# Mixer modulation split between TensorE and VectorE, in a hybrid decoder block on one Trainium2 core

## The chip, the core and the metric

The kernel runs on one core of one Trainium2 chip. Its five engines run their own instruction queues in order: TensorE (PE, with its weight loads as PEld), VectorE (DVE), ScalarE (ACT), GpSimd (POOL) and SyncE (SP), which here issues nearly all DMAs. The metric is device microseconds of one execution; lower is better.

## The reference

One decoder layer with adaptive normalisation over 512 tokens of width D = 2048, all in float32:

```python
mod = silu(c) @ w_ada + b_ada          # c: one row of 2048; w_ada: 2048 x 6*2048
sh_a, sc_a, g_a, sh_m, sc_m, g_m = split(mod, 6)
h    = rmsnorm(x, norm_mix_g) * (1 + sc_a) + sh_a
proj = h @ w_in                        # q_a k_a v_a | q_b k_b v_b f_b
...                                    # sliding-window and forgetting attention, w_out, two-level MoE, final norm
```

What matters here are the first two of the six sections of `mod`, the mixer's shift and scale: a row of 2048 times a 2048 x 4096 part of w_ada, 33.5 MB that are read once. Every column of h, and with it every row of w_in that is multiplied, waits for its own shift and scale.

## The kernel before

The first 150 us are one pipeline over the 2048 columns of h. The columns are cut into 8 "u" of 256, and these into UNITS ((0,1), (1,3), (3,5), (5,7), (7,8)). For each unit (loop over UNITS, L410):

- `gemv(u0, u1)` forms shift (sec 0) and scale (sec 1) of the unit's columns. For each section it loads w_ada in four row chunks kc (tiles `raws`, 1 MB each, five buffers in rotation, two of them the buffers of x) and multiplies each by silu(c) with 16 matmuls in four column groups of 32 (L318, `gv`). Silu(c) is the stationary operand, so all 32 rows of a group hold the same sum. ACT copies `gv` to `row` (L324), PE picks one row of each group, adds the four and turns them into columns (`cp`, L330), and VectorE writes shA (L332) or scA (L334, L335).
- `make_h(u0, u1)` scales the columns of x (already transposed in `xT`) by scA and by the token norm `rsb` (VectorE, L341), ACT adds the shift and rounds to the high part hT_hi (L342), VectorE forms the low part hT_lo (L345). Two column blocks k of 128 belong to each u.
- `start_proj(u0, u1)` is the projection of the finished unit: six steps for each u (two for the K piece of w_in, four for the Q piece), each step six matmuls of 512 columns (high x high, high x low, low x high, L211 to L213). A piece is fetched with `ws.get()`, which also issues loads ahead and lets ACT and VectorE cut the next piece into high and low parts (L172/L173 for K, L178/L179 for Q).

The projection of a unit runs inside the gemv of the next one: gemv is a generator that yields after each kc (yield 1) and after the copy of `row` (yield 0), and at each yield the loop takes n steps of `prev`, the projection of the unit before. What is left is emitted behind make_h. So the order on PE and on VectorE is written out by hand: an instruction that waits holds everything behind it on its engine. After the last unit, the K accumulators are copied out by ACT (L471, L472), and attention starts.

Before the units, `begin()` (L251) loads and transposes x, forms the token norms and spreads them over the partitions (`rb`, copied to `rsb` by ACT, L277); `columns()` (L279) transposes the small vectors (`vt`, copied to `vecs` by VectorE at L284, then `gps`, which uses the same PSUM bank).

Of the kernel before, what the change touches and what calls it, by code (L numbers as in the profile page):

```python
# [8 lines left out]
F32 = mybir.dt.float32  # L9
# [44 lines left out]
def kernel(  # L54
# [8 lines left out]
    V, S, G, PE, SP = nc.vector, nc.scalar, nc.gpsimd, nc.tensor, nc.sync  # L63
# [19 lines left out]
    big = ctx.enter_context(tc.tile_pool(name="big", bufs=1))  # L83
    frt = ExitStack()
    fr = frt.enter_context(tc.tile_pool(name="front", bufs=1, side="right"))
    att = ExitStack()
    sb = att.enter_context(tc.tile_pool(name="start", bufs=1))
    pst = ExitStack()
    ps = pst.enter_context(tc.tile_pool(name="ps0", bufs=1, space=PSUM, reuse_waits="tile"))
# [15 lines left out]
    ones = ones1.to_broadcast([128, 128])  # L105
    sel4 = big.tile([128, 1], F32, name="sel4")
    V.memset(sel4, 0.0)
    for q in range(4):
        V.memset(sel4[32 * q:32 * q + 1, :], 1.0)
    csig = big.tile([128, 4, 4], F32, name="csig")  # L110
    S.activation(csig, ccol, AF.Exp, scale=-1.0)
    V.tensor_scalar(csig, csig, 1.0, None, op0=OP.add)
    V.reciprocal(csig, csig)
    csil = big.tile([128, 4, 4], F32, name="csil")
    V.tensor_mul(csil, ccol, csig)
    cs32 = big.tile([128, 16, 32], F32, tag="wr", name="cs32")
    V.tensor_copy(cs32, flat(csil)[:, :, None].to_broadcast([128, 16, 32]))

    shA = big.tile([128, 16], F32, name="shA")
    scA = big.tile([128, 16], F32, name="scA")  # L120
# [3 lines left out]
    def rsqrt_(dst, v, tmp):  # L124

        S.activation(tmp, v, AF.Sqrt)
        V.reciprocal(dst, tmp)
        V.tensor_mul(tmp, dst, dst)
        V.tensor_mul(tmp, tmp, v)
        V.tensor_scalar(tmp, tmp, -0.5, 1.5, op0=OP.mult, op1=OP.add)  # L130
        V.tensor_mul(dst, dst, tmp)  # L131
# [83 lines left out]
    hT_hi = fr.tile([128, 4, 4, T], F32R, tag="B", name="hT_hi")  # L215
    hT_lo = [big.tile([128, 4 * n, T], F32R, tag=f"C{i}", name=f"hT_lo{i}") for i, n in enumerate((3, 1))]

    def kt(ts, k, sl=slice(0, T)):

        return ts[k // 12][:, k % 12, sl]  # L220
# [10 lines left out]
    xT = [sb.tile([128, 4, T], F32, name=f"xT{i}") for i in range(4)]  # L231
    rsb = fr.tile([128, T], F32, tag="gacc1", name="rsb", bufs=1)
# [18 lines left out]
    def begin():  # L251

        for tb in range(TB):
            SP.dma_start(xt[tb], x[tb * 128:(tb + 1) * 128, :])
        scr = fr.tile([128, 2, 1024], F32, tag="ga", name="sqscr")
        for tb in range(TB):
            V.tensor_tensor_reduce(scr[:, 0], xt[tb][:, :1024], xt[tb][:, :1024], scale=1.0, scalar=0.0, op0=OP.mult,
                                   op1=OP.add, accum_out=sx2[:, tb, 0:1])
            S.activation(scr[:, 1], xt[tb][:, 1024:], AF.Square, accum_out=sx2[:, tb, 1:2])
            for i in range(4):  # L260
                tr = ps.tile([128, 4, 128], F32, tag=f"acc{(4 * tb + i) % 6}", name=f"xTp_{tb}_{i}")
                for j in range(4):
                    k = 4 * i + j
                    PE.transpose(tr[:, j, :], xt[tb][:, k * 128:(k + 1) * 128], ident)
                o = xT[i][:, :, tb * 128:(tb + 1) * 128]
                if i % 2:
                    V.tensor_copy(o, tr)
                else:
                    S.activation(o, tr, AF.Copy)
        V.tensor_reduce(ssx, sx2, axis=AX.X, op=OP.add)  # L270
        V.tensor_scalar(ssx, ssx, 1.0 / D, EPS, op0=OP.mult, op1=OP.add)
        rsqrt_(rsx, ssx, tsx)
        rb = ps.tile([128, T], F32, tag="tr", name="rb")
        for tb in range(TB):
            PE.matmul(rb[:, tb * 128:(tb + 1) * 128], rsx[:, tb:tb + 1].to_broadcast([128, 128]), ident,
                      start=tb == 0, stop=tb == TB - 1)
        S.activation(rsb, rb, AF.Copy)  # L277

    def columns():  # L279

        vt = ps.tile([128, 2, 24], F32, tag="tr", name="vt")
        for j in range(2):
            PE.transpose(vt[:, j, :], vrow[:, 128 * j:128 * j + 128], ident[:24, :24])
        V.tensor_copy(vecs.rearrange("p n (u j) -> p n u j", j=2), vt.rearrange("p j (n u) -> p n u j", n=3))  # L284
        gps = ps.tile([128, 16], F32, tag="tr", name="gps")
        PE.transpose(gps, grow, ident[:16, :16])
        V.tensor_copy(gout, gps)


    UNITS = ((0, 1), (1, 3), (3, 5), (5, 7), (7, 8))  # L290
    nraws = [0]

    def raws():

        n = nraws[0]
        nraws[0] += 1
        tag = f"raws{n % 3}" if n < 4 else ("raws1", "raws2", "A0", "A1", "raws0")[(n - 4) % 5]
        pool = sb if tag[0] == "r" else big
        return pool.tile([128, 4, 512], F32, tag=tag, name="raws", bufs=1)

    def gemv(u0, u1):

        n = 256 * (u1 - u0)
        ks = slice(2 * u0, 2 * u1)
        per = 512 // n
        for sec, dst in ((0, shA), (1, scA)):
            gv = ps.tile([128, 512], F32, tag="gv", name=f"gv_{sec}_{u0}")[:, :n]
            cols = slice(sec * D + u0 * 256, sec * D + u1 * 256)
            for kc in range(4):
                if kc % per == 0:  # L310
                    t = raws().rearrange("p a (b f) -> p (a b) f", f=n)
                    for i in range(2):
                        if per == 2:
                            SP.dma_start(t[:, 4 * i:4 * i + 4], rows4(w_ada, kc + i)[:, :, cols])
                        else:
                            SP.dma_start(t[:, 2 * i:2 * i + 2], rows4(w_ada, kc)[:, 2 * i:2 * i + 2, cols])
                for q in range(4):
                    PE.matmul(gv[32 * q:32 * q + 32, :], cs32[:, kc * 4 + q, :], t[:, kc % per * 4 + q, :],  # L318
                              start=kc == 0, stop=kc == 3)
                if sec and kc in (1, 3):  # L320
                    ws.ahead(2 * u0 + 2 if kc == 1 else 2 * u1)
                yield 1
            row = sb.tile([128, 512], F32, tag="bias", name=f"row_{sec}_{u0}", bufs=2)[:, :n]
            S.activation(row, gv, AF.Copy)  # L324
            if sec == 1 and u0 == 0:
                ws.split(2)
            yield 0
            cp = ps.tile([128, 512], F32, tag="tr", name=f"cp_{sec}_{u0}")[:, :n // 128]
            for k in range(n // 128):
                PE.matmul(cp[:, k:k + 1], row[:, k * 128:(k + 1) * 128], sel4, start=True, stop=True)  # L330
            if sec == 0:
                V.tensor_add(shA[:, ks], cp, vecs[:, 0, ks])  # L332
            else:
                V.scalar_tensor_tensor(scA[:, ks], cp, 1.0, vecs[:, 1, ks], op0=OP.add, op1=OP.add)  # L334
                V.tensor_mul(scA[:, ks], scA[:, ks], gmix[:, ks])  # L335

    def make_h(u0, u1):
        for k in range(2 * u0, 2 * u1 + 1):
            if k < 2 * u1:
                v = xT[k // 4][:, k % 4, :]  # L340
                V.scalar_tensor_tensor(v, v, scA[:, k:k + 1], rsb, op0=OP.mult, op1=OP.mult)  # L341
                S.activation(hT_hi[:, k // 4, k % 4, :], v, AF.Identity, bias=shA[:, k:k + 1])  # L342
            if k > 2 * u0:
                i, j = divmod(k - 1, 4)
                V.scalar_tensor_tensor(kt(hT_lo, k - 1), xT[i][:, j, :], shA[:, k - 1:k], hT_hi[:, i, j, :].bitcast(F32),  # L345
                                       op0=OP.add, op1=OP.subtract)

    WO = tuple((lambda cc=cc, n=n: wout_load(cc, n), False)
               for cc, ns in ((0, range(4)), (1, range(4)), (2, range(8)), (0, range(4, 8)), (1, range(4, 8)), (3, range(8)))
# [33 lines left out]
    ws = Stream(items)  # L383
# [25 lines left out]

    for g, us in enumerate(UNITS):  # L410
        if g == 1:
            S.dma_start(bfg, bcast(b_forget, 16))
            S.dma_start(sinkb, bcast(sinks, 16))
        if g == 0:
            begin()
            columns()
            acc0 = [ps.tile([128, 512], F32, tag=f"acc{i}", name=f"acc0_{i}") for i in range(6)]

        free = 6 * (UNITS[g - 1][1] - UNITS[g - 1][0]) - 4 if g else 0
        loads = 0  # L420
        for kc in gemv(*us):
            loads += kc
            n = 1
            if kc:
                n = free * loads // 8 - free * (loads - 1) // 8
            for _ in range(n):
                next(prev, None)
        make_h(*us)
        for _ in prev:
            pass  # L430
        prev = start_proj(*us)
# [795 lines left out]
    for tb in range(TB):  # L1227
        for k in range(tb + 1):
            PE.matmul(rk[:, tb, :], before if k == tb else ones_b, chosen_b[:, k].rearrange("p g e -> p (g e)"),
                      start=k == 0, stop=k == tb)  # L1230
# [468 lines left out]
```

## Time and profile before

| | us |
|---|---|
| median of 3 runs | 1908.92 |
| lowest, highest | 1907.39, 1909.3 |
| the profiled execution | 1906.88 |
| its span, first to last instruction | 1904.9 |
| PE busy in the span | 1811.7 (95%) |
| DVE busy | 1017.2 (53%) |
| ACT busy | 747.3 (39%) |

Times inside the kernel are us from the start of the span. The stretch that the change touches ends at 152; the rest of the span (attention, output projection, MoE) is untouched. "Granted clock" is the share of TensorE's full clock that it was given: 1.00 is 2.4 GHz, 0.50 is 1.2 GHz.

### The profile page before, as it was taken

How to read it: one execution, taken by the hardware profiler on the slowest of the kernel's cores; microseconds unless marked ns; L12 is line 12 of the kernel's file. 1: busy time of each engine (PE TensorE's matmuls, PEld its weight loads, DVE VectorE, ACT ScalarE, POOL GpSimd, SP SyncE). 2: the span in 40 equal slices, each digit the busy share in tenths (PEclk: the TensorE clock that was granted, in tenths of full speed). 3: DMA queues.
4: the chain of work that ended last, by engine and by line, in shares of the span. 5: the costliest groups of instructions: out<-in, count | busy, mean ns of one | idle time of the engine just before them, and what ended most of it. 6: DMA issues, size and time to landing. Idle time of an engine off the chain costs nothing.

```text
span 1904.9 us, 25988 instructions
## 1 busy us (share of the span) xinstructions
PE 1811.7 (95%) x9777; PEld 1130.0 (59%) x9777; DVE 1017.2 (53%) x1799; ACT 747.3 (39%) x1450; POOL 289.1 (15%) x217
## 2 busy tenths in 40 slices
PE   7998999999999999998899999999999999999995
PEld 4467888788777777777544454444444445444432
DVE  3334666666666544756645464444554545545435
ACT  3225656565565543345533232232331323323213
POOL 0000334444345241355000000000000000000000
PEclk8999999999999999999899999999999999999998
DMA  9963555565656332667899999999999999999995
GB/s 338 384 229 75 156 182 151 159 212 156 188 172 188 122 133 67 219 206 288 347 363 387 419 420 420 420 419 419 419 418 420 414 420 419 418 420 416 420 412 214
DMA packets 196501, 573.81 MB, mean 301 GB/s; under 512 B 22624, under 2 KB 86152, under 8 KB 147600
## 3 DMA queue, kind: packets, MB, share of 16 engines
q1 hardware_dynamic: 195456, 572.00, 79.3%
q8 instruction: 79, 1.29, 0.3%
q14 instruction: 54, 0.44, 0.1%
q10 hardware_dynamic: 912, 0.07, 0.0%
HBM read 567.82 MB, written 4.19 MB: 300 GB/s over the span
## 4 chain that ended last, share of the span: by engine, by line
PE 75%; DMA 8%; DVE 7%; ACT 6%; issue 3%; POOL 0%; SPq 0%; ACTq 0%; DVEq 0%; POOLq 0%
PE pu L1334 12%; PE pg L1334 11%; PE y L1356 9%; PE xe L1467 7%; PE o L1378 5%; DMA w<-in_w_up_dram 4%; PE qp L211 3%; PE qp L213 2%; PE qp L212 2%; DMA raw<-in_w_ada_dram 2%; PE acc L211 1%; PE gv L318 1%; PE acc L212 1%; PE acc L213 1%; PE ob L813 1%
## 5 line engine op out<-in xcount | busy, mean ns | idle before, releaser
L1334 PE MATMUL pu<-w,cw 128*64 128x512 f32 x1024 | 239.2, 593 | 5.4 <-DMA w<-in_w_up_dram 5.4
L1334 PE MATMUL pg<-w,cw 128*64 128x512 f32 x1024 | 236.2, 598 | 0.7 <-DMA w<-in_w_gate_dram 0.7
L1476 ACT ACTIVATE cw<-xe,shM,scM 128x128 f32<-128x128 f32 x128 | 58.5, 457 | 430.9 <-PE xe L1467 399.9
L1356 PE MATMUL y<-w,more_f 128*64 128x512 f32 x960 | 212.6, 594 | 4.3 <-ACT xp_whi L1448 2.4
L1474 DVE TENSOR_SCALAR cw<-xe,scM,shM 128x128 f32<-128x128 f32 x128 | 52.5, 410 | 300.7 <-ACT cw L1476 300.7
L612 POOL TENSOR_TENSOR gb<-gb,raw 128x512 f32<-128x512 f32 x112 | 162.2, 1448 | 276.1 <-ACT raw L611 210.8
L1381 DVE SCALAR_TENSOR_TENSOR x<-o,wpair,x 128x512 f32<-128x512 f32 x240 | 163.2, 743 | 19.4 <-PE o L1378 19.4
L1334 PEld LDWEIGHTS pu<-w,cw 128*64 128x64 f32 x1024 | 75.8, 137 | 154.0 <-issue 141.2
L1448 ACT ACTIVATE xp_whi<-x,rs 128x256 fp32r<-128x256 f32 x236 | 162.4, 761 | 1.1 <-DVE rs L131 1.1
L1356 PEld LDWEIGHTS y<-w,more_f 128*64 128x64 f32 x960 | 71.5, 137 | 132.8 <-issue 107.1
L1334 PEld LDWEIGHTS pg<-w,cw 128*64 128x64 f32 x1024 | 71.7, 136 | 131.4 <-issue 126.9
L173 DVE TENSOR_TENSOR wlo_s<-raw,whi_s 128x512 fp32r<-128x512 f32 x96 | 91.5, 954 | 107.2 <-ACT whi_s L172 107.0
L1454 DVE SCALAR_TENSOR_TENSOR xp_wlo<-x,rs,xp_whi 128x256 fp32r<-128x256 f32 x232 | 144.6, 682 | 2.2 <-ACT xp_whi L1448 2.2
L1467 PE MATMUL xe<-cr,xp_whi 128*128 128x256 f32 x472 | 121.9, 296 | 2.4 <-DVE cr L1437 2.4
L609 DVE SCALAR_TENSOR_TENSOR ga<-raw,csil,ga 128x512 f32<-128x512 f32 x112 | 109.5, 978 | 25.2 <-DMA raw<-in_w_ada_dram 24.7
L1467 PEld LDWEIGHTS xe<-cr,xp_whi 128*128 128x128 f32 x472 | 89.9, 190 | 49.5 <-issue 45.4
L1467 PE MATMUL xe<-cr,xp_wlo 128*128 128x256 f32 x472 | 115.6, 283 | 0.0
L211 PE MATMUL qp<-hT_hi,whi_s 128*128 128x512 f32 x256 | 107.7, 421 | 0.0
L213 PE MATMUL qp<-hT_hi,wlo_s 128*128 128x512 f32 x256 | 100.8, 394 | 0.0
L212 PE MATMUL qp<-hT_lo,whi_s 128*128 128x512 f32 x256 | 100.8, 394 | 0.0
L611 ACT ACTIVATE raw<-raw,csil 128x512 f32<-128x512 f32 x112 | 79.7, 713 | 31.8 <-DMA raw<-in_w_ada_dram 29.8
L1467 PEld LDWEIGHTS xe<-cr,xp_wlo 128*128 128x128 f32 x472 | 90.1, 191 | 0.0
(440 smaller groups left out, 3366.1 us busy)
## 6 DMA issues: line engine op xcount, KB each, us to landing
w<-in_w_gate_dram SPq DMA_DIRECT2D x128, 1024.0 KB, 10.7
w<-in_w_up_dram SPq DMA_DIRECT2D x128, 1024.0 KB, 14.0
w<-in_w_down_dram SPq DMA_DIRECT2D x126, 1024.0 KB, 10.3
raw<-in_w_ada_dram SPq DMA_DIRECT2D x128, 512.0 KB, 3.9
raws<-in_w_ada_dram SPq DMA_DIRECT2D x64, 512.0 KB, 10.2
raw<-in_w_in_dram SPq DMA_DIRECT2D x160, 128.0 KB, 3.0
raw<-in_w_out_dram SPq DMA_DIRECT2D x32, 512.0 KB, 3.8
raw<-in_w_in_dram SPq DMA_DIRECT2D x48, 256.0 KB, 3.6
```

What stands on the lines that cost most here:

```text
L211: PE.matmul(o, lhi, rhi, start=first, stop=False, **kw)
L212: PE.matmul(o, lhi, rlo, start=False, stop=False, **kw)
L213: PE.matmul(o, llo, rhi, start=False, stop=last, **kw)
L609: V.scalar_tensor_tensor(a, ts[n][:, j, :], s, a, op0=OP.mult, op1=OP.add)
L612: G.tensor_add(a, a, ts[n][:, j, :])
L1334: PE.matmul(o[64 * e:64 * e + 64, :], self.xe(cc)[:, j, 64 * e:64 * e + 64], w[cc, e][:, j, :], start=cc == 0 and j == 0, stop=cc == 3 and ...
L1356: PE.matmul(ys[dc][64 * e:64 * e + 64, :], HT[:, k, 64 * e:64 * e + 64], self.wd[k, e][:, dc, :], start=k == 0, stop=k == 3)
L1378: PE.matmul(o, self.ohT[:, tb, :], v, start=i == 0, stop=i == 1)
L1381: V.scalar_tensor_tensor(x2, o, self.w_col(tb), x2 if self.n else x1[dc][:, tb, :], op0=OP.mult, op1=OP.add)
L1448: S.activation(hi[tb], xv, AF.Identity, scale=s)
L1454: V.scalar_tensor_tensor(lo[tb], xv, s, hi[tb].bitcast(F32), op0=OP.mult, op1=OP.subtract)
L1467: PE.matmul(t[:, j, :], v[tb][:, j, :], OHS[:, tb].rearrange("p q s -> p (q s)"), start=tb + i == 0, stop=tb + i == TB)
```

## The change

For every unit but the first, the row chunks kc 0 and 1 are no longer multiplied on PE. VectorE multiplies each of their eight 128-row slices by the matching column of silu(c) and adds it up in a tile `sums`; PE adds `sums` over the partitions, 128 columns in each of up to four column groups (`st`, stationary operand ones), ACT copies that too, and one more matmul with `pick4` brings it into `cp`. So half of the multiplication by silu(c) moves from PE to VectorE, eight slices for each section.

UNITS becomes ((0,1), (1,3), (3,5), (5,6), (6,7), (7,8)). `raws` rotates over seven buffers, all four of x among them. The steps of the projection are dealt out by another rule: one at each yield as long as more than one is left, two of them kept for the yields 0. For a previous unit of two u it is one at each of the eight yields 1, one at each yield 0 and two behind make_h; for one u, a step at the first three yields 1, one at each yield 0, one behind make_h.

x is multiplied by the token norm ahead, in four VectorE instructions of 128x2048 in `norm_row()`, which with `columns()` now stands behind the first section of the first unit. make_h then needs one tensor_scalar (scale and shift together), one ACT copy and one subtraction for each k.

```diff
@@ begin / norm_row
+    def norm_row():
         rb = ps.tile([128, T], F32, tag="tr", name="rb")
...
         S.activation(rsb, rb, AF.Copy)
+        for i in range(4):
+            V.tensor_mul(xT[i], xT[i], rsb[:, None, :].to_broadcast([128, 4, T]))
@@
-    UNITS = ((0, 1), (1, 3), (3, 5), (5, 7), (7, 8))
+    UNITS = ((0, 1), (1, 3), (3, 5), (5, 6), (6, 7), (7, 8))
...
-        tag = f"raws{n % 3}" if n < 4 else ("raws1", "raws2", "A0", "A1", "raws0")[(n - 4) % 5]
+        tag = f"raws{n % 3}" if n < 4 else ("A0", "raws1", "A1", "raws2", "A2", "raws0", "A3")[(n - 4) % 7]
@@ gemv
+        se = 2 if u0 else 0
...
                 for q in range(4):
-                    PE.matmul(gv[32 * q:32 * q + 32, :], cs32[:, kc * 4 + q, :], t[:, kc % per * 4 + q, :],
-                              start=kc == 0, stop=kc == 3)
-                if sec and kc in (1, 3):
-                    ws.ahead(2 * u0 + 2 if kc == 1 else 2 * u1)
-                yield 1
+                    v = t[:, kc % per * 4 + q, :]
+                    if kc >= se:
+                        PE.matmul(gv[32 * q:32 * q + 32, :], cs32[:, kc * 4 + q, :], v, start=kc == se, stop=kc == 3)
+                    elif kc or q:
+                        V.scalar_tensor_tensor(sums, v, csil[:, kc, q:q + 1], sums, op0=OP.mult, op1=OP.add)
+                    else:
+                        V.tensor_scalar(sums, v, csil[:, 0, 0:1], None, op0=OP.mult)
+                if kc < 3:
+                    yield 1
+            st = ps.tile([128, 132], F32, tag="tr", name=f"st_{sec}_{u0}")
+            w = 32 * nk
+            for k in range(nk if se else 0):
+                PE.matmul(st[32 * k:32 * k + 32, :128], ones[:, 0:32], sums[:, k * 128:(k + 1) * 128], start=True, stop=True)
+            if sec:
+                ws.ahead(2 * u1)
+            yield 1
...
+            if se:
+                S.activation(row[:w, 512:], st[:w, :128], AF.Copy)
...
+            cp = st[:, 128:128 + nk]
+            if se:
+                PE.matmul(cp, row[:w, 512:], pick4[:w, :nk], start=True, stop=False)
+            for k in range(nk):
+                PE.matmul(cp[:, k:k + 1], row[:, k * 128:(k + 1) * 128], sel4, start=not se, stop=not se or k == nk - 1)
@@ make_h
-                V.scalar_tensor_tensor(v, v, scA[:, k:k + 1], rsb, op0=OP.mult, op1=OP.mult)
-                S.activation(hT_hi[:, k // 4, k % 4, :], v, AF.Identity, bias=shA[:, k:k + 1])
+                V.tensor_scalar(v, v, scA[:, k:k + 1], shA[:, k:k + 1], op0=OP.mult, op1=OP.add)
+                S.activation(hT_hi[:, k // 4, k % 4, :], v, AF.Copy)
...
-                V.scalar_tensor_tensor(kt(hT_lo, k - 1), xT[i][:, j, :], shA[:, k - 1:k], hT_hi[:, i, j, :].bitcast(F32),
-                                       op0=OP.add, op1=OP.subtract)
+                V.tensor_sub(kt(hT_lo, k - 1), xT[i][:, j, :], hT_hi[:, i, j, :].bitcast(F32))
@@ the loop over UNITS
-        free = 6 * (UNITS[g - 1][1] - UNITS[g - 1][0]) - 4 if g else 0
+        left = 6 * (UNITS[g - 1][1] - UNITS[g - 1][0]) - 2 if g else 0
         loads = 0
         for kc in gemv(*us):
             loads += kc
-            n = 1
-            if kc:
-                n = free * loads // 8 - free * (loads - 1) // 8
+            if g == 0 and kc and loads == 4:
+                norm_row()
+                columns()
+            n = (left + 8 - loads) // (10 - loads) if kc else 1
+            left -= n if kc else 0
             for _ in range(n):
                 next(prev, None)
```

## Rows read from the trace of the kernel before

**Rows 1.** Windows of the first stage: us, then each engine's busy us; PEclk, DMA share, GB/s.
```profile
20.00:37.00 17.00, 13.92 (x91) 5.63 (x91) 4.47 (x11) 4.06 (x8) 0.00 (x0) 0.51 0.96 321
37.00:58.00 21.00, 16.57 (x75) 5.20 (x70) 1.80 (x4) 1.60 (x4) 0.00 (x0) 0.99 1.06 382
58.00:120.00 62.00, 62.00 (x336) 37.22 (x335) 22.27 (x39) 16.77 (x27) 0.00 (x0) 1.00 1.06 378
120.00:152.00 32.00, 32.00 (x182) 21.95 (x180) 13.59 (x25) 13.31 (x23) 2.03 (x7) 1.00 0.25 65
```
**Rows 2.** Timeline of PE: start us, us, what; last data of unit (1,3), its scale.
```profile
56.73 1.05 PE L318 MATMUL gv<-raws,cs 128*32 128x512 f32 x4 [0.32 <-DMA raws<-in_w_ada_dram]
...
60.61 0.95 PE L330 MATMUL cp<-sel,row 128*128 128x1 f32 x8
```
**Rows 3.** Timeline of PE: gemv blocks and projection steps, later, and the end of the stage.
```profile
76.87 1.06 PE L318 MATMUL gv<-raws,cs 128*32 128x512 f32 x8
...
79.46 1.06 PE L318 MATMUL gv<-raws,cs 128*32 128x512 f32 x8
...
122.35 0.64 PE L318 MATMUL gv<-raws,cs 128*32 128x256 f32 x8
...
124.50 0.64 PE L318 MATMUL gv<-raws,cs 128*32 128x256 f32 x8
...
145.10 0.39 PE L211 MATMUL acc<-hT_hi,hi_s 128*128 128x512 f32 x1
...
146.49 0.39 PE L211 MATMUL acc<-hT_hi,hi_s 128*128 128x512 f32 x1
...
155.74 0.39 PE L211 MATMUL vaa<-hi_s,hT_hi 128*128 128x272 f32 x1 [3.60 <-ACT hi_s L172]
```
**Rows 4.** Timeline of VectorE: make_h of unit (3,5), and a Q piece behind it.
```profile
89.50 0.16 DVE L334 SCALAR_TENSOR_TENSOR scA<-cp,vecs 128x4 f32<-128x4 f32 x1 [3.64 <-PE cp L330]
...
89.89 1.42 DVE L341 SCALAR_TENSOR_TENSOR xT<-xT,scA,rsb 128x512 f32<-128x512 f32 x2
91.44 0.75 DVE L345 SCALAR_TENSOR_TENSOR hT_lo<-xT,shA,hT_hi 128x512 fp32r<-128x512 f32 x1
...
95.64 1.28 DVE L179 TENSOR_TENSOR lo_s<-raw,hi_s 128x512 fp32r<-128x512 f32 x2
```
**Rows 5.** Groups by line and shape of VectorE, 0 to 200 us: busy us, mean ns.
```profile
L607 DVE TENSOR_SCALAR ga<-raw,csil 128x512 f32<-128x512 f32 x1 | 0.5, 481 | 0.0
```
**Rows 6.** Timeline of VectorE, later: a 1024-wide subtraction; two dependent instructions.
```profile
860.26 1.22 DVE L173 TENSOR_TENSOR lo_s<-raw,hi_s 128x1024 fp32r<-128x1024 f32 x1
...
889.06 0.69 DVE L1095 TENSOR_TENSOR gx<-oq,ga 128x512 f32<-128x512 f32 x1 [1.28 <-PE oq L213]
889.79 0.69 DVE L1096 TENSOR_TENSOR x<-x,gx 128x512 f32<-128x512 f32 x1
```
**Rows 7.** Timeline of all engines: token norm, small vectors and gemv of the first unit.
```profile
20.20 0.60 ACT L277 ACTIVATE rsb<-rb 128x512 f32<-128x512 f32 x1 [2.26 <-PE rb L275]
...
21.56 0.28 PE L286 MATMUL gps<-ident,grow 16*128 16x16 f32 x1 [0.30 <-DVE vecs L284]
21.77 3.64 PE L318 MATMUL gv<-raws,cs 128*32 128x256 f32 x32
...
31.89 0.38 ACT L324 ACTIVATE row<-gv 128x256 f32<-128x256 f32 x1 [6.02 <-PE gv L318]
...
34.63 0.15 DVE L334 SCALAR_TENSOR_TENSOR scA<-cp,vecs 128x2 f32<-128x2 f32 x1
```
**Rows 8.** Windows (columns as in rows 1): the clock behind the pause that ends at 155.74.
```profile
157.00:158.00 1.00, 1.00 (x6) 1.00 (x5) 0.59 (x2) 0.97 (x2) 0.00 (x0) 0.50 0.37 53
...
161.00:162.00 1.00, 1.00 (x10) 1.00 (x9) 0.99 (x2) 0.78 (x2) 0.00 (x0) 1.00 0.00 0
```
**Rows 9.** Timeline of PE: a later pause.
```profile
189.16 0.39 PE L211 MATMUL vb<-whi_s,hT_hi 128*128 128x256 f32 x1 [2.80 <-ACT whi_s L172]
```
**Rows 10.** Windows: the clock behind that pause.
```profile
191.00:192.00 1.00, 1.00 (x7) 1.00 (x7) 0.74 (x4) 0.43 (x2) 0.00 (x0) 0.50 0.78 222
```

More of the change, by code (lines that the diff above doesn't have):

```diff
@@ L109 @@
         V.memset(sel4[32 * q:32 * q + 1, :], 1.0)
+    pick4 = big.tile([128, 4], F32, name="pick4")
+    V.memset(pick4, 0.0)
+    for q in range(4):
+        V.memset(pick4[32 * q:32 * q + 1, q:q + 1], 1.0)
     csig = big.tile([128, 4, 4], F32, name="csig")
@@ L304, in gemv @@
         ks = slice(2 * u0, 2 * u1)
-        per = 512 // n
+        per, nk = 512 // n, n // 128
+        se = 2 if u0 else 0
         for sec, dst in ((0, shA), (1, scA)):
             gv = ps.tile([128, 512], F32, tag="gv", name=f"gv_{sec}_{u0}")[:, :n]
+            if se:
+                sums = fr.tile([128, 2048], F32, tag="ga", name=f"sums_{sec}_{u0}")[:, :n]
             cols = slice(sec * D + u0 * 256, sec * D + u1 * 256)
@@ L317, in gemv @@
                 for q in range(4):
-                    PE.matmul(gv[32 * q:32 * q + 32, :], cs32[:, kc * 4 + q, :], t[:, kc % per * 4 + q, :],
-                              start=kc == 0, stop=kc == 3)
-                if sec and kc in (1, 3):
-                    ws.ahead(2 * u0 + 2 if kc == 1 else 2 * u1)
-                yield 1
-            row = sb.tile([128, 512], F32, tag="bias", name=f"row_{sec}_{u0}", bufs=2)[:, :n]
-            S.activation(row, gv, AF.Copy)
+                    v = t[:, kc % per * 4 + q, :]
[14 more added lines that the diff above has]
+            yield 1
+            row = sb.tile([128, 640], F32, tag="bias", name=f"row_{sec}_{u0}", bufs=2)
+            S.activation(row[:, :n], gv, AF.Copy)
+            if se:
+                S.activation(row[:w, 512:], st[:w, :128], AF.Copy)
             if sec == 1 and u0 == 0:
@@ L327, in gemv @@
             yield 0
-            cp = ps.tile([128, 512], F32, tag="tr", name=f"cp_{sec}_{u0}")[:, :n // 128]
-            for k in range(n // 128):
-                PE.matmul(cp[:, k:k + 1], row[:, k * 128:(k + 1) * 128], sel4, start=True, stop=True)
+            cp = st[:, 128:128 + nk]
+            if se:
+                PE.matmul(cp, row[:w, 512:], pick4[:w, :nk], start=True, stop=False)
+            for k in range(nk):
+                PE.matmul(cp[:, k:k + 1], row[:, k * 128:(k + 1) * 128], sel4, start=not se, stop=not se or k == nk - 1)
             if sec == 0:
@@ L415 @@
             begin()
-            columns()
             acc0 = [ps.tile([128, 512], F32, tag=f"acc{i}", name=f"acc0_{i}") for i in range(6)]
-        free = 6 * (UNITS[g - 1][1] - UNITS[g - 1][0]) - 4 if g else 0
+        left = 6 * (UNITS[g - 1][1] - UNITS[g - 1][0]) - 2 if g else 0
         loads = 0
```

## The prediction

> **What bounds the kernel now.** I read the windows first, since the change touches only the first 152 us. Up to 37 PE has gaps and a granted clock of 0.51; from 37 to 58 the DMA share is 1.06 and PE is busy 16.6 of 21.0 us; from 58 on PE has no gap, to 120 with DMA full as well, from 120 to 152 with DMA at 0.25 [rows 1]. So DMA sets the time up to the last data of unit (1,3), at 56.7 [rows 2], and PE alone from there to its last projection matmul at 152.1, 3.6 before 155.74 [rows 3]. VectorE is busy 22.3 of 62 us there [rows 1]: it looks free for more, and the question is whether its new work comes in time, because PE and VectorE both run in the order written. All later work follows the K accumulators through ACT, so I carry a shift of this stage to the end of the program in full.
>
> The anchor is the matmuls `cp` for the scale of unit (1,3): they start at 60.6 and end at 61.4 [rows 2]; before, the stage needs 152.1 - 61.4 = 90.7 us from there.
>
> **Prices of PE.** A step is 146.49 - 145.10 = 1.39. A 512-wide gemv block between steps costs 79.46 - 76.87 - 1.39 = 1.20, a 256-wide one 124.50 - 122.35 - 1.39 = 0.76 [rows 3]. `cp` for four columns costs about 0.9 [rows 2], for two half of it, 0.45. New in each section: the `st` matmuls, 128 wide, next to a gemv block in the same column groups. Half the width saves 0.44, so a quarter of the width would be about 0.55 with the switch to and from column groups and less without: I take 0.35, between 0.1 and 0.55. The matmul with `pick4` is one of the eight-for-0.9 kind, two passes, 0.2.
>
> **What PE loses and gains behind the anchor.** Unit (3,5): two sections, each without two blocks and with 0.55 more: 2 x (2.40 - 0.55) = 3.7 saved. Before, (5,7) costs 8 x 1.20 + 2 x 0.9 = 11.4; as (5,6) and (6,7) it costs four sections of 2 x 0.76 + 0.55 + 0.45 = 2.5, 10.1: 1.3 saved. Unit (7,8): 8 x 0.76 + 0.9 = 7.0 becomes 5.0: 2.0 saved. One projection step now lies ahead of the anchor: 1.4. Together 8.4 us less PE work; if PE never waited, the stage would end that much earlier.
>
> **Prices of VectorE.** Two instructions that don't depend on each other start 0.67 apart though each takes 0.75 [rows 4]; two that do start 0.73 apart at 0.69 each, the duration and 0.04 [rows 6]. Every addition to `sums` reads the one before, so I take 0.79 for 512 columns. The first of a section is a tensor_scalar, 0.48 [rows 5]. A 512-wide section: 0.52 + 7 x 0.79 = 6.05 (by 0.67 it would be 5.2). For 256 columns, half of the step from 0.69 to 1.22 between 512 and 1024 [rows 4, 6] comes off, 0.27: 0.52 each, 4.0 for a section (3.1 by the lower price). The Trainium skill, VectorE: DVE Perf Modes (section The DRAIN you can't avoid) says that the next instruction does not start until the pipe is empty; by that any two would be a full 0.75 apart. The pair in the trace at 0.67 shows that this holds only for dependent ones here; the sum would go by 5.8 a section.
>
> make_h gets shorter. Before, from scA to the end of the fourth low part: 95.6 - 89.5 = 6.1 [rows 4]. After, the tensor_scalar takes 0.48 (lower bound nothing, upper bound 0.75 as now), and the chain scale, ACT copy, subtraction gives the first low part 2.3 after `cp` (before, 92.2 - 89.5 = 2.7 behind the start of scA alone [rows 4]) and the fourth about 4.9 after it.
>
> **Where PE waits.** VectorE's order for a unit is: make_h, slices of kc 0, cutting of the Q piece that the first step asks for (1.28 [rows 4]), slices of kc 1. PE's order: two or one left steps, step 1, step 2, block kc 2, step 3, block kc 3, `st`. Step 3 needs the Q piece and `st` needs kc 1. Times in us behind the `cp` of the scale before:
> - Unit (3,5), shift: make_h ends at 4.9, kc 0 at 7.8, Q at 9.1, kc 1 at 12.3. PE has one left step and waits for the first low part until 2.3; then step 1 and 2 and a block, 6.3; step 3 waits to 9.2; with block kc 3 it is at 11.8, and `st` waits 0.5. Waits: 0.9 + 2.9 + 0.5. The scale section has enough steps: no wait.
> - Unit (5,6), shift: four k in make_h still, narrow slices. Kc 0 ends at 6.9, Q at 8.2; two left steps, two steps and a block end at 6.3: wait 1.9. Then none.
> - Units (6,7) and (7,8): the unit before has six steps only, three go to the first three yields, one to each yield 0, one behind make_h. In the scale section VectorE can't begin before the `cp` of the shift, because the addition into shA stands ahead of kc 0 in its queue; it needs 0.2 + 4.0. PE has two blocks, 1.25, and no step: it waits 2.95 at `st`. Behind `cp` of the scale there is one step (1.39) against the 2.3 of the chain: 0.9. So 3.85 in each, 7.7, and this happens because (5,7) is cut in two and the steps are dealt early.
> Sum: 4.3 + 1.9 + 7.7 = 13.9 us of new waits against 8.4 us saved: the stage behind the anchor becomes 5.5 us longer.
>
> **The anchor itself.** In the first unit, the four multiplications by rsb stand ahead of the copy `vecs`, and PE's transpose `gps`, `cp` and the whole scale section stand behind that copy. One is 128x2048: 512 to 1024 adds 0.53 [rows 4, 6], so 2048 is about 2.3, 2.2 apart, 8.9 for four. They can begin when `rb` is copied, which now stands behind the first section's gemv: about 22.7, against 20.8 for the copy before [rows 7]; this lies between 21 and 25, as the landing of that section's data isn't shown. They end at 31.6, `cp` at 33.4, and the scale section at the clock of 0.51 takes as the one before, 3.64 [rows 1, 7]: 37.0 against 31.9 before, 5 us later. From there to scA 2.74 [rows 7], and the first step can run at about 42, on a half clock at first. The shift section of (1,3) then gets to its `cp` at about 53; VectorE's 6.2 for the scale section end at 59.3, where before only the data were waited for (56.7). With `st`, a step and `cp` the anchor ends at 62.3 (59 to 66): 0.9 later. The DMA queue has no part in it: seven buffers, and the fourth tile no longer waits for `vecs`, so the data come earlier if anything, by 3 us at most.
>
> **Costed at nothing.** The ACT copies of `st` (under the step at yield 0), `pick4` (at the very start, before c has landed), the later `ws.ahead` (each `get` loads ahead too; the DMAs are the same in number and bytes, and are passed by no others in SP's queue). If that cover fails, a 0.4 us copy would show twelve times at worst.
>
> Sum: 5.5 + 0.9 = 6.4, and for the clock 1.6 (below, one stretch of it): **+8 us**. The profiled execution has 1904.9 of span and 1906.9 in all, 2 us under the median of 1908.9; so it would give 1915, and the median **1917 us**.
>
> **The rivals.**
> *PE stays fed* (faster). The additions to `sums` take 0.67 or less and are out of PE's way, or waits fall where PE would wait for DMA anyway; PE's 8.4 are then won, less the 0.9 of the anchor: 1901. For it: VectorE has two thirds of its time free [rows 1]. Against it: nothing in the code lets PE pass a waiting `st`. It decides if the slices of a scale section end before PE's two blocks, and the row of 0.48 for a tensor_scalar is far from that.
> *Waits and savings cancel* (no change). With 0.67 for 0.79 and the anchor at 61.4 or earlier, the waits shrink by about 0.9 in each of five places and the sum is near +2; 1911, between 1906 and 1912.
> *The clock falls in the waits* (slower still). A pause of 3.6 us is followed by a clock of 0.50 (1.2 GHz) from 157 that is back at 1.00 (2.4 GHz) by 161 [rows 3, 8], one of 2.8 us by 0.50 at 191 [rows 9, 10]; the pauses that I expect are 2.9 to 3 four times, and about 3.5 in (1,3). A stretch of three to four us at half the clock costs 1.6. The Trainium skill, TensorE: Matmul & The Clock Gate (Part 1), has the throttled state as the default that activity lifts; the rows agree, and the change takes activity away. One such stretch is in my forecast; four or five give +14: 1923.
> *The change does not do what it says* is excluded for the sums: the matmuls of kc 0 and 1 are gone from the code.
>
> **Chances.** Forecast, slower by 4 to 12: 0.44. Clock: 0.18. Cancelled: 0.20. Fed: 0.18. The range from 1903 to 1924 takes in the first and third whole, most of the second, and stops short of the fed case at its full size; that leaves out about 2 in 10. A measurement can tell about 0.2%, 4 us, from no change: faster 0.18, same 0.20, slower 0.62.
>
> **What would show it.** PE's last projection matmul moves from 152 to 158 to 162. Right: VectorE's additions to `sums` about 0.79 apart; PE idle some 3 us before `st` in the scale sections of (6,7) and (7,8), ended by VectorE; step 3 of (3,5) held by the cutting of Q; four long multiplications from about 23 to 32 with PE idle. Wrong: PE without a gap from 60 on (then the fed case), additions 0.67 or less apart, or an anchor before 58.

## The result: 14 us slower, and the profile after

| | before | after |
|---|---|---|
| median | 1908.16 | 1922.39 |
| lowest, highest | 1906.0, 1909.3 | 1920.37, 1926.67 |
| the profiled execution | 1906.88 | 1921.61 |
| its span | 1904.9 | 1919.4 |

The ratio is 1.0079 with a 95% interval of [1.0059, 1.0099]. Forecast were 1917 and slower; the sign was right, the size too small by 5 to 6 us, and the sum behind it splits otherwise than forecast: less work saved, more half clock, a later anchor. Of the runs further down, one of e1 (6285.58) and one of e2 (6522.55) fell into a slow state; the ratios leave them out, the medians have them in (without them 1906.07 and 1909.69).

The windows of the kernel after (us, then the busy us of PE, PEld, DVE, ACT, POOL; PEclk, DMA share, GB/s):

```profile
20.00:37.00 17.00, 7.20 (x51) 4.53 (x55) 9.35 (x7) 0.98 (x2) 0.00 (x0) 0.60 1.07 372
37.00:58.00 21.00, 15.90 (x90) 9.04 (x82) 14.29 (x24) 5.08 (x10) 0.00 (x0) 0.76 0.97 343
58.00:120.00 62.00, 55.30 (x295) 36.83 (x296) 40.47 (x75) 15.82 (x32) 0.00 (x0) 0.94 0.88 300
120.00:152.00 32.00, 24.90 (x155) 15.66 (x153) 21.30 (x47) 6.80 (x15) 0.54 (x2) 0.95 0.66 205
152.00:166.00 14.00, 13.75 (x50) 10.63 (x51) 5.80 (x13) 5.90 (x11) 1.72 (x5) 0.76 0.09 21
```

Against [rows 1]: PE, without a gap from 58 to 152 before, has 6.7 and 7.1 us of them now; the DMA share from 58 on falls from 1.06 to 0.88, and PEclk is no longer 1.00. The loads fall because SP, which issues them in order, waits for VectorE. At L155 it waits for the buffer of a piece of w_in, which comes free when VectorE has cut the piece in it; these cuts stand in VectorE's queue between and behind the sums, and where the list names the sums there, they are what VectorE had last in hand, since no sum reads such a buffer. At L327 it waits for a buffer of w_ada from which VectorE still adds up. Waits of SP's queue for VectorE from 58 to 120 (line and releaser, us in total, times, longest):

```profile
SPq L155 <- DVE lo_s L183: 14.8, 3, 7.4
SPq L155 <- DVE sums L333: 8.4, 1, 8.4
SPq L327 <- DVE sums L333: 5.5, 2, 3.4
```

With two smaller ones, 3.6 and 1.6, they come to 33.9 us; before, such waits are 1.6 us in the same window.

The end of the stage shows all of the loss. Timeline of PE, the first block behind the stage (before: 155.74 [rows 3]):

```profile
171.54 0.39 PE L215 MATMUL vaa<-hi_s,hT_hi 128*128 128x272 f32 x1 [3.51 <-ACT hi_s L176]
```

It is 15.8 later, the profiled execution 14.7 longer. I call this time "the first vaa block" below.

What PE waited for from the anchor to its last projection matmul (line waited for: us in total, times, longest), and the same stretch as one window:

```profile
PE st L342 <- DVE sums L333: 7.6, 3, 3.4
PE acc L217 <- DVE lo_s L183: 2.7, 2, 1.8
PE acc L215 <- ACT hT_hi L369: 0.6, 2, 0.3
PE acc L216 <- DVE hT_lo L372: 0.5, 2, 0.2
...
65.20:168.00 102.80, 91.24 (x482) 60.61 (x480) 65.27 (x130) 30.21 (x59) 2.26 (x7) 0.93 0.67 220
```

The same window of the kernel before, 61.6 to 152.2, has PE busy 90.55 of 90.6. The four stretches at low clock from 58 on:

```profile
60.00:64.00 4.00, 3.52 (x17) 2.64 (x17) 0.34 (x1) 0.28 (x1) 0.00 (x0) 0.58 1.06 388
74.00:78.00 4.00, 3.84 (x21) 1.11 (x21) 3.89 (x6) 0.49 (x1) 0.00 (x0) 0.57 1.05 388
132.00:136.00 4.00, 3.34 (x11) 2.11 (x11) 0.48 (x1) 0.28 (x1) 0.00 (x0) 0.57 1.10 348
152.00:160.00 8.00, 7.75 (x25) 5.78 (x26) 2.93 (x8) 2.16 (x5) 1.72 (x5) 0.57 0.00 0
```

PE's busy time times (1 - PEclk) is an estimate of what the clock cost in each: 1.5, 1.7, 1.4 and 3.3. So the stretch from anchor to end can be split. It grew from 90.6 to 102.8, by **12.2**: 11.6 of gaps, 6.4 of half clock (the last three), less the work saved, 90.55 - (91.24 - 6.4) = 5.7. The rest of the 15.8 is the anchor, scA of unit (1,3) at 65.16 where it stood at 61.59: **3.6**.

How a wait at `st` arises is seen in unit (6,7). Timeline of DVE, then of PE:

```profile
128.40 0.16 DVE L359 TENSOR_TENSOR shA<-st,vecs 128x2 f32<-128x2 f32 x1 [2.49 <-PE st L357]
128.51 0.35 DVE L335 TENSOR_SCALAR sums<-raws,csil 128x256 f32<-128x256 f32 x1
128.90 3.61 DVE L333 SCALAR_TENSOR_TENSOR sums<-raws,csil,sums 128x256 f32<-128x256 f32 x7
...
128.22 1.07 PE L331 MATMUL gv<-raws,cs 128*32 128x256 f32 x16
132.66 0.64 PE L342 MATMUL st<-sums,ones 128*32 128x128 f32 x4 [3.36 <-DVE sums L333]
```

VectorE stands idle for 2.49 because the addition into shA is next in its queue and PE has not made `cp` yet; the eight slices stand behind it, and once it is done they run without a wait for data. PE then has two blocks to do, is through at 129.3 and waits 3.36. In (7,8) the same row stands at 152.25, again with 3.36.

### The profile page after: what moved, and what is told of

It is laid out like the page before. It is cut to its first block, busy times and chain, and to the rows that moved or that the text cites. A ratio compares the mean times of both kernels' runs of the same rounds, so it can differ in the third digit from the quotient of the medians.

```text
span 1919.4 us, 26096 instructions
## 1 busy us (share of the span) xinstructions
PE 1812.4 (94%) x9757; PEld 1139.8 (59%) x9757; DVE 1063.9 (55%) x1891; ACT 749.0 (39%) x1462; POOL 288.6 (15%) x217
## 4 chain that ended last, share of the span: by engine, by line
PE 70%; DMA 9%; DVE 9%; ACT 7%; issue 3%; POOL 1%; SPq 0%; DVEq 0%; ACTq 0%; POOLq 0%
PE pu L1361 12%; PE pg L1361 11%; PE y L1383 9%; PE xe L1494 7%; PE o L1405 5%; DMA w<-in_w_up_dram 4%; PE qp L215 2%; PE qp L217 2%; PE qp L216 2%; DMA raw<-in_w_ada_dram 2%; DMA raws<-in_w_ada_dram 1%; DVE sums L333 1%; PE ob L840 1%; DMA raw<-in_w_in_dram 1%; PE tb L828 1%
## 5 line engine op out<-in xcount | busy, mean ns | idle before, releaser
L636 DVE SCALAR_TENSOR_TENSOR ga<-raw,csil,ga 128x512 f32<-128x512 f32 x112 | 106.4, 950 | 24.9 <-DMA raw<-in_w_ada_dram 24.4
```

The costliest lines, as they stand in the source:

```text
L636: V.scalar_tensor_tensor(a, ts[n][:, j, :], s, a, op0=OP.mult, op1=OP.add)
```

## The experiments

Theories: **A**, VectorE's sums come late, PE waits for them and goes on at half clock; **B**, the cut of (5,7) and the new dealing of steps cost the time, whichever engine sums; **C**, scaling x ahead delays the first unit. **D** came later: the loads bound the stretch as well. All kernels start from the kernel after. The table collects what follows (us; the ratio, with its interval, is to the runs of the kernel before that were taken with each, of medians 1908.03 to 1908.65; the last three columns are of each profiled execution: scA of (1,3), the first vaa block, and the way from one to the other).

| kernel | sums on | units | median | ratio | anchor | block | way |
|---|---|---|---|---|---|---|---|
| before | PE | old | 1908.16 | 1 | 61.59 | 155.74 | 94.2 |
| after | DVE | new | 1922.39 | 1.0079 [1.0059, 1.0099] | 65.16 | 171.54 | 106.4 |
| e1, e12 | PE | new | 1906.33, 1906.72 | 0.9984 [0.9971, 0.9997], 0.9992 [0.9981, 1.0004] | 59.54 | 154.14 | 94.6 |
| e2 | DVE | old | 1910.96 | 1.0016 [1.0002, 1.0029] | 65.56 | 160.07 | 94.5 |
| e3 shift late | DVE | new | 1907.54 | 0.9999 [0.9987, 1.0011] | 62.02 | 159.59 | 97.6 |
| e4 32/26/26 fillers | DVE | new | 1929.05 | 1.0110 [1.0091, 1.0128] | 67.60 | 175.90 | 108.3 |
| e7 17/13/13 fillers | DVE | new | 1923.20 | 1.0084 [1.0068, 1.0101] | 62.58 | 165.68 | 103.1 |
| e8 columns first | DVE | new | 1916.53 | 1.0049 [1.0033, 1.0066] | 58.01 | 166.14 | 108.1 |
| e5 shift late | DVE | old | 1905.97 | 0.9994 [0.9983, 1.0004] | 60.96 | 155.01 | 94.1 |
| e6 = e5, columns and Q first | DVE | old | 1908.22 | 1.0003 [0.9988, 1.0019] | 59.36 | 158.15 | 98.8 |
| e9 = e5, columns first | DVE | old | 1903.61 | 0.9978 [0.9968, 0.9988] | 58.44 | 152.44 | 94.0 |
| e10 columns first | PE | new | 1903.69 | 0.9978 [0.9968, 0.9988] | 57.59 | 152.56 | 95.0 |
| e11 columns first | PE | old | 1902.43 | 0.9967 [0.9953, 0.9980] | 57.71 | 150.94 | 93.2 |

In e3 and e7 the profiled execution is not a middle one (1913.74 and 1913.35 us).

### Which of the three parts it is: e1, e12, e2

```diff
-        se = 2 if u0 else 0
+        se = 0
```

> The changed kernel with all four row chunks of every section back on TensorE: no sums on VectorE, no st matmuls, no pick4. Units, dealing of the steps, seven buffers and x scaled ahead stay. Theory A (VectorE's sums come late and TensorE waits for them, then runs at half clock): TensorE has no wait longer than about 1 us behind unit (1,3); it pays 16 blocks of 0.76 and four cp of 0.45 for (5,7) cut in two in place of 11.4, so 2.6 more, and saves one step of 1.4 behind the anchor: +1 to +3 against before, about 1910. Rival B (the cut of (5,7) and the early dealing of the steps cost the time, whichever engine sums): they are still there, so +8 or more, 1916 and up. Rival C (x scaled ahead delays the first unit and everything follows): the anchor, scA of unit (1,3), stays at 65 where it was 61.6 before: +4 to +6, 1913.

1906.33. The rows are from the same kernel run once more:

> e1_all_on_pe once more, for its rows, since its profile was disturbed: 1906, with the anchor (scA of (1,3)) at 61 to 63, TensorE busy over 0.97 of 58 to 120, no wait for sums, and half-clock stretches as in the kernel before (10 us of TensorE's time up to 200) or fewer.

1906.72, with the anchor 1.5 earlier than expected; scA of (1,3) on VectorE and the window that holds the last 60 us before 120:

```profile
59.54 0.16 DVE L361 SCALAR_TENSOR_TENSOR scA<-st,vecs 128x4 f32<-128x4 f32 x1 [5.77 <-PE st L357]
...
60.00:120.00 60.00, 60.00 (x353) 35.92 (x352) 21.96 (x41) 16.92 (x30) 0.00 (x0) 1.00 1.04 352
```

With the cut, the dealing, the seven buffers and the scaling ahead all kept, the loss is gone, and PE has no gap up to 120. B falls as stated (it expected 1916 or more), and C as the cause of the whole. The way is that of before within 0.5.

```diff
-    UNITS = ((0, 1), (1, 3), (3, 5), (5, 6), (6, 7), (7, 8))
+    UNITS = ((0, 1), (1, 3), (3, 5), (5, 7), (7, 8))
```

> The changed kernel with the units of before, (5,7) whole again; sums on VectorE, dealing and x ahead stay. Theory A: the two units in which the unit before has only six steps are gone behind the anchor; (5,7) waits like (3,5), some 3.4, and (7,8) some 1.9, and 10.8 are saved on TensorE against 9.6 of waits; with an anchor 3.6 late and one stretch of half clock: +2 to +5 against before, about 1912. Rival B: the cause is taken away, 1908 or less. Rival C: the start is as late as in the changed kernel and nothing else counts: 1920 and up.

1910.96, a ratio that stands for 3 us, as A expected (2 to 5). The way is back at 94.5; what is left against before is the anchor, 4.0 late. So neither the sums on VectorE nor the cut costs the 12 us of the way: the two together do, because behind a unit of one u there are too few steps, and PE comes to `st` with two blocks and no step before it.

### The order on VectorE: e3

In e3 the shift section's `cp` and its addition into shA are emitted behind kc 1 of the scale section, so that the slices of kc 0 and 1 stand ahead of them. PE's `pick4` and `cp` move with the addition, so PE's order changes as well.

```diff
+                if kc == 2 and late:
+                    late.pop()()
                 for q in range(4):
...
+            if se and sec == 0:
+                late.append(to_columns)    # pick4, cp, shA as before
+            else:
+                to_columns()
```

> The changed kernel, but cp and the addition into shA of the shift section are emitted only behind kc 1 of the scale section, so that VectorE can begin the scale section's sums as soon as st of the shift section has read the tile. Nothing is left out. Theory A: the waits before st of the scale section, 4.1 in (1,3) and 3.4 in (6,7) and (7,8), shrink to about 1 each, and the half clock behind them (1.6, 1.5 and 3.2) goes: 10 to 14 us less than the changed kernel, 1908 to 1912. Rival B: the order on VectorE does not matter, 1920 and up. Rival C: at most the 4 of unit (1,3) come back, 1918.

1907.54: nearly all of the 14 us from one reordering without a change of work. PE's waits at `st` from 58 to 168 in the kernel after, then its waits in e3:

```profile
PE st L342 <- DVE sums L333: 11.7, 4, 4.1
```

```profile
PE acc L217 <- DVE lo_s L183: 2.7, 2, 1.8
PE st L345 <- DVE shA L365: 2.6, 3, 1.1
PE st L345 <- DVE sums L336: 2.4, 2, 1.5
```

No wait is above 1.8, where the kernel after has three of 3.4 to 4.1 at `st` in (1,3), (6,7) and (7,8); and from 50 to 158 PEclk stays at 1.00. The waits and the half clock go together, and the order of the queues makes both.

### The clock by itself: e4, e7

Matmuls of the identity with itself are put ahead of `st` in the scale sections of (1,3), (6,7) and (7,8), where PE would stand idle. They change nothing in the output: `st` overwrites what they write.

```diff
+            for _ in range({1: 32, 6: 26, 7: 26}.get(u0, 0) if sec else 0):
+                PE.matmul(st[:, :128], ident, ident, start=True, stop=True)
```

> The changed kernel with 32, 26 and 26 matmuls of ident by ident (128 columns, into st, which the real sums overwrite) ahead of st in the scale sections of (1,3), (6,7) and (7,8), to fill the waits there; no other change. If TensorE's half clock at 61 to 64, 132 to 136 and 153 to 159 comes from its pauses, the granted clock stays at 1.00 there and 1.6 + 1.5 + 3.2 = 6 us come back: about 1916. If the slow matmuls there have another cause, nothing comes back, or some tenths are lost: 1922 to 1923.

1929.05, a miss: I had taken a filler for half of what it is. 52 instructions (two passes each of 26) took 6.07 us in place of a pause of 3.4, 2.7 more than had been idle there. The block comes 4.4 later than in the kernel after; the profiled execution is 7.8 longer, and the 3.4 us behind the block stay unexplained. Filler and `st` on PE, and windows of e4:

```profile
131.60 6.07 PE L342 MATMUL st<-ident 128*128 128x128 f32 x52
137.60 0.41 PE L344 MATMUL st<-sums,ones 128*32 128x128 f32 x4
...
129.00:133.00 4.00, 4.00 (x38) 2.98 (x37) 2.08 (x6) 0.38 (x1) 0.00 (x0) 1.00 1.11 344
133.00:142.00 9.00, 8.94 (x64) 7.47 (x63) 3.10 (x8) 0.74 (x2) 0.00 (x0) 1.00 0.84 259
142.00:165.00 23.00, 21.69 (x145) 15.91 (x146) 13.92 (x29) 5.87 (x13) 2.26 (x7) 1.00 0.10 25
```

As a reading of the clock it worked: with PE kept at work, 129 to 165 is at 1.00 (2.4 GHz), where the kernel after has two stretches at 1.2 GHz. Behind the wait of 1.8 at step 3 of (3,5), which e4 has as well, it is at 1.00 too (69 to 90). The Trainium skill, TensorE: Matmul & The Clock Gate (Part 1), says that the throttled state is the default and activity lifts it; these rows agree.

e7 has 17, 13 and 13 of them.

> As the run with filler matmuls, whose 32, 26 and 26 fillers took 7.4, 6.1 and 6.1 us (0.23 each) where 4.1, 3.4 and 3.4 were to be filled: now 17, 13 and 13, 3.9, 3.0 and 3.0 us. Clock theory: the granted clock stays at 1.00 behind the three waits and the half-clock stretches of the changed kernel (1.6, 1.5 and 3.2 us lost) do not come: 5 to 6 us less than the changed kernel, 1916 to 1918. If the slow stretches have another cause than the pauses: 1922 or more.

Not settled. The profiled execution took 1913.35, 8.3 under the profiled one of after, with the block 5.9 earlier and PEclk 1.00 from 125 to 165; the four others took 1918.53 to 1923.53, and there is no trace of them. That fillers can buy the half clock off and save about 6 us up to the block is shown in one execution, not in the median.

### The anchor: e8

```diff
+    def scale_x():
         for i in range(4):
             V.tensor_mul(xT[i], xT[i], rsb[:, None, :].to_broadcast([128, 4, T]))
...
                 columns()
+                scale_x()
```

> The changed kernel with the four multiplications of x by the token norm emitted behind the small vectors, so that TensorE's transpose and the first unit's scale section no longer wait for them; nothing else. Theory A with the late anchor as a part: scA of the first unit comes at about 35.5 in place of 40.7, VectorE's sums of (1,3) start 5 earlier, and the anchor, scA of (1,3), comes at about 60 in place of 65.2: about 5 us less than the changed kernel, 1917. If the data or other work set the anchor: 1921 to 1922.

1916.53, as expected. In the kernel after the multiplications and the copy behind them were

```profile
23.65 8.90 DVE L285 TENSOR_TENSOR xT<-xT,rsb 128x2048 f32<-128x2048 f32 x4 [4.84 <-ACT rsb L283]
32.47 0.20 DVE L292 COPY vecs<-vt 128x48 f32<-128x48 f32 x1
```

and PE's `gps` waited 8.8 us for it. With the order turned, scA of unit 0 comes at 34.0 instead of 40.7, the anchor at 58.0 instead of 65.2 and the block 5.4 earlier. C holds for this part of the loss, which e2 has as well, but only with the sums on VectorE: e12 has the same wait of PE, 8.8, and its anchor is at 59.54.

### Can the savings be had at all: e5, e6, e9, e10, e11

> The changed kernel with the units of before and with cp and the addition into shA behind kc 1 of the scale section, both together. Theory A: against the kernel with the old units alone (1911) the wait of 3.7 before st in (1,3) and the half clock behind it (about 3) go; the waits for the cut of the Q piece (1.3 in the mean, three times) and for the first high parts stay: 1903 to 1906, faster than before. If what is taken from one wait is given back by the next: 1908 to 1911.

e5 joins e2 and e3: 1905.97. The half clock behind the anchor is gone, and of the waits are left 4.0 at `st` and 3.2 at step 3 (three each, none over 1.5). PE is busy 54.1 of the 60 us up to 120 where it was busy throughout, and yet the way is 94.1, as before.

> As the run with the old units and the late shift, and in addition the Q piece that the first step asks for is cut ahead of the sums of kc 0, and the small vectors go ahead of the multiplications of x. Theory A: the waits for the cut pieces (3.6 in sum with the old units) go, and the first unit comes 5 earlier, of which the data of (1,3) leave 2 at most: 3 to 5 less than the run without the two, 1899 to 1902. If VectorE only moves its lateness from the piece to the sums, st waits longer and nothing is won: as that run.

e6 (e5, with columns first, and `ws.split(ws.n + 2)` ahead of each gemv, so that Q is cut before the slices) gave 1908.22, a miss. Its DVE timeline in the shift section of (5,7), and its waits at `st` from 20 to 175, below them the same of e9 (waits from 20 to 150):

```profile
93.70 1.29 DVE L183 TENSOR_TENSOR lo_s<-raw,hi_s 128x512 fp32r<-128x512 f32 x2
94.91 0.48 DVE L340 TENSOR_SCALAR sums<-raws,csil 128x512 f32<-128x512 f32 x1
95.42 5.48 DVE L338 SCALAR_TENSOR_TENSOR sums<-raws,csil,sums 128x512 f32<-128x512 f32 x7
...
PE st L347 <- DVE sums L338: 8.9, 3, 3.4
```

```profile
91.64 2.33 DVE L338 SCALAR_TENSOR_TENSOR sums<-raws,csil,sums 128x512 f32<-128x512 f32 x3
93.88 1.28 DVE L183 TENSOR_TENSOR lo_s<-raw,hi_s 128x512 fp32r<-128x512 f32 x2
95.08 3.10 DVE L338 SCALAR_TENSOR_TENSOR sums<-raws,csil,sums 128x512 f32<-128x512 f32 x4
...
PE st L347 <- DVE sums L338: 3.9, 3, 1.5
```

VectorE is packed there: what the cut gains for step 3 (3.7 of waits in e9, none in e6), the sums lose at `st` (8.9 against 3.9). A wait was moved and made longer, not removed, and from 60 to 120 e6 is at a PEclk of 0.94, e9 at 1.00.

> The late shift section and the old units of e5_late_old (1905.97), with the small vectors turned to columns ahead of the four multiplications as in e8_columns_first, but Q's piece cut where the change cuts it; e6_late_old_q_cols had this and the earlier cut and won nothing (1908.2, first vaa block at 158.15 against 155.01 for e5). Theory A (TensorE's waits and the late anchor are the whole matter): unit 0's scA falls from 41.28 to 34.4 as in e6, the anchor from 60.96 to 57, and the first vaa block comes at 150 to 151: 1901 to 1902. Theory D (the loads bound the stretch too: in e5_late_old the DMA engines are at 1.05 to 1.10 of their time from 60 to 120, at 385 GB/s, and drop to 0.5 right behind 120): columns first lifts the traffic of 20 to 60 from 355 to 377 GB/s, 40 us x 22 GB/s = 0.9 MB or 2.3 us at 385 GB/s, and no more is to be had: first vaa block at 152.5 to 153, 1903.5 to 1904. If it was not the earlier cut that cost e6 its gain, the block stays at 158 and the time at 1908.

> All sums back on TensorE as in e1_all_on_pe (1906.3), and the small vectors turned to columns ahead of the four multiplications. Theory A: with nothing late from VectorE, unit 0's scA falls by 6, TensorE is the bound from there on, and what it starts 6 us earlier ends up to 6 us earlier: 1900 to 1902. Theory D: the loads bound the stretch, the traffic of 20 to 60 rises by 22 GB/s, and 2.3 us are won: 1904. If TensorE's own work of 20 to 37 fills the place anyway: 1906.

> As e10_on_pe_cols, with the units of before (1024 columns of (5,7) in one). In e1_all_on_pe the cut into (5,6) and (6,7) cost nothing to be seen; but with six units each section of 256 columns has its own modulation and row on TensorE, about 1.4 for the additional section pair. Theory B says that these 1 to 2 us come back: 1 to 2 below e10. Theory A and theory D: within 1 of e10.

e9, with Q back in its place, gave 1903.61 and the block at 152.44: the numbers of D (152.5 to 153; 1903.5 to 1904), not of A (150 to 151); and it was the earlier cut that had cost e6 its gain. e10 gave 1903.69, D's 1904 again. The windows of e5, e9 and e11, in this order:

```profile
60.00:120.00 60.00, 54.12 (x300) 36.29 (x300) 43.55 (x75) 16.69 (x32) 0.00 (x0) 1.00 1.06 379
```

```profile
20.00:60.00 40.00, 26.93 (x163) 15.31 (x163) 26.99 (x38) 6.93 (x15) 0.00 (x0) 0.83 1.06 377
60.00:120.00 60.00, 53.76 (x302) 35.95 (x302) 44.57 (x75) 18.20 (x35) 0.00 (x0) 1.00 1.06 375
```

```profile
20.00:60.00 40.00, 30.88 (x183) 14.55 (x183) 16.40 (x24) 7.16 (x13) 0.00 (x0) 0.87 1.06 377
60.00:120.00 60.00, 60.00 (x336) 34.73 (x332) 21.81 (x42) 16.85 (x29) 0.00 (x0) 1.00 1.06 374
```

e9 and e11 differ in the engine that sums and in the late shift that goes with it. PE is busy 53.8 us in one and 60.0 in the other, at full clock; the DMA engines are full in both, at the same rate, and the blocks stand 1.5 apart, the kernel with more PE work being the earlier one. The Trainium skill, DMA: Bandwidth & Descriptors (Specifications), has the fabric's ceiling at 435 GB/s and one core's limit at the HBM at about 358; the 374 to 379 of these rows, at a share of 1.06, lie between the two, so the second did not bind here.

A full share does not say that anything waited for a load. PE's waits say that. They follow for e9, from 20 to 150, with PE's busy time from the anchor to the last projection matmul, where the kernel before has 90.55 of 90.55:

```profile
PE gv L336 <- DMA raws<-in_w_ada_dram: 5.0, 4, 2.8
PE st L364 <- DVE shA L367: 4.7, 1, 4.7
PE st L347 <- DVE sums L338: 3.9, 3, 1.5
PE acc L217 <- DVE lo_s L183: 3.7, 3, 1.5
...
58.44:148.92 90.48, 82.29 (x446) 56.43 (x445) 61.73 (x111) 29.42 (x55) 2.23 (x7) 1.00 0.79 272
```

The waits for loads all lie ahead of the anchor; the longest, 2.8, ends at 50.49, in the scale section of (1,3). There D holds: against e5, scA of unit 0 comes 6.8 earlier, but the anchor only 2.5 and the block 2.6. Behind the anchor neither PE nor VectorE waits for a load in e9. PE has 8.3 us less work than before and 8.2 us of gaps, all of them for VectorE: 3.9 at `st`, 3.7 for the cut of Q at step 3, the rest at first steps; e5 has 7.7 less and 7.7 of gaps. So the way is no shorter than before because the waits that are left give back what the work saves, and not because the loads hold it. D's number for the block was right by the anchor; its reason does not hold behind it. Whether the loads would be next if these waits went too is not shown: no kernel here with its sums on VectorE is without them, and none with fewer bytes was run.

From 120 to 152 e9 has 4.9 us of gaps; 3.1 of them belong to the pause ahead of the first vaa block, which every kernel has.

**e11 beats both kernels:** sums on PE, old units, x scaled ahead behind the small vectors, seven buffers, 1902.43. Its distance to e10, 1.3, is what B said of the old units (1 to 2), but it lies within the intervals, so it is not shown.

## Why the prediction was right in sign and short in size

- **Where the time shows.** Right in place, not in size. The last projection matmul moved from 152.1 to 168.0 (forecast 158 to 162), and what lies behind the block is unchanged within 1.1.
- **VectorE's prices.** Right. Seven dependent additions of 512 columns took 5.48 and three 2.33, so they start 0.79 apart (forecast 0.79); of 256 columns 3.61 and 1.52, 0.52 apart (0.52); the first of a section took 0.48 and 0.35.
- **PE's price.** 8.4 saved was forecast; at full clock it is 5.7. `gv` fell from 22.2 to 12.4 us in the stretch, but `cp`, `pick4` and `st` rose from 4.8 to 12.7 (part of it at half clock): for eight sections `st` took 3.6, 0.45 each (forecast 0.35), `pick4` 3.0 (forecast 1.6), `cp` 6.1 where the same 40 matmuls had been 4.8 in six sections.
- **The waits.** Right in mechanism and place: the addition into shA ahead of the slices in (6,7) and (7,8), Q's cut at step 3 of (3,5) and the first steps behind make_h; the 1.9 of (5,6) came as 0.9 at step 3 and 0.9 at `st`. Forecast were 13.9 in all; measured 11.6, with the two at `st` at 3.36 each instead of 2.95 and step 3 at 1.8 instead of 2.9.
- **The clock.** This is the step that was mis-sized: "One such stretch is in my forecast". Between anchor and end there are three, 6.4 us in place of 1.6, and one more, 1.5, ahead of the anchor. The rival *the clock falls in the waits* had four or five, at 1923, and is what came: there are four, behind the waits of 4.07, 1.77, 3.36 and 3.36. I gave it 0.18. That its 1923 lies so near the 1922.39 is in part luck, since two other errors, in PE's price and in the waits, nearly cancel.
- **The anchor.** Forecast +0.9, measured +3.6. (Before, `cp` ends at 60.61 + 0.95 = 61.56 [rows 2], not at the 61.4 of the prediction; the forecast would have been +0.7.) The four multiplications were right to 0.01 (8.90 for 8.9; from 23.65, inside 21 to 25). Unit 0's scA came at 40.7 for 39.7, and the sums of (1,3) end at 60.3 for 59.3: that is 1.0 of the missing 2.7, and the low clock from 60 on is 1.5.
- **What bounds the kernel.** "PE alone from there" is borne out: behind the anchor neither PE nor VectorE waits for a load in the kernels before and after, though the DMA share is 1.06 beside PE's 62.0 of 62 up to 120 [rows 1]. The rival *PE stays fed* was met by no run. The saving that it counts on is there once the cut of (5,7) is taken back, 7.7 in e5 and 8.3 in e9, but so are 7.7 and 8.2 us of waits for VectorE: with the old units the outcome is that of *Waits and savings cancel*, though not by its cheaper additions: some 8 us of waits came where 13.9 were forecast for the new units.

The sum of the three errors behind the anchor is 4.8 (clock) + 2.7 (PE's price) - 2.3 (waits) = 5.2; with 2.7 of the anchor it is 7.9, and 8 + 7.9 is, but for rounding, the 15.8 by which the block moved.

## What to carry to other kernels

Two resources at full share in one window do not tell which of them holds the time; the waits do. Here the DMA engines were full up to 120 and nothing behind the anchor waited for them, while the work that PE lost came back as its waits for VectorE. In queues that are written by hand, a small instruction that waits for another engine must stand behind the work that needn't wait: moving one addition, with the matmuls that feed it, was worth 15 us here. Price a wait of TensorE with the half clock that may follow it, and count one such stretch for each long wait, not one for all: the three waits of 3.4 to 4.1 each had one; behind waits of 1.4 to 1.8, e3, e4, e5 and e9 have none.

## What the runs showed of the hardware

- The clock took up to as much again as the wait itself: behind two pauses of 3.36 each, 1.4 and 3.3 us were lost at half of it. The length of one wait doesn't settle it: the stretch at 74 to 78 stands behind one of 1.77, and e3 and e4 have one of 1.8 with no drop behind it.
- An fp32 matmul of 128 columns on the whole array comes as two passes and took 0.23 (6.07 for 26), as much as lies between the starts of two matmuls of a projection step with 512 columns (1.39 for six [rows 3]).
- Narrow units load worse at the same share. From 20 to 120, e11 (old units) and then e10 (new ones, otherwise the same):

```profile
DMA packets 23707, 37.54 MB, mean 375 GB/s; under 512 B 1499, under 2 KB 9363, under 8 KB 23699
```

```profile
DMA packets 26674, 36.18 MB, mean 362 GB/s; under 512 B 1714, under 2 KB 16426, under 8 KB 26666
```

The cut of (5,7) turns rows of 2 KB into rows of 1 KB (512 and 256 columns of 4 bytes). From 60 to 120 the DMA engines are full in both (1.06 and 1.05) and move 374 and 351 GB/s; from 20 to 120, 1.36 MB less arrive, which is 3.6 us at 375 GB/s. PE waits for none of it behind the anchor.
